# Attention units of two heads by 256 queries, with P times V in the two column halves

## The chip, the core and the metric

The kernel runs on one core of a Trainium2 chip. Its time is the device time in microseconds (us) of that core; a smaller number is better. The kernel before was run three times: 4213.78, 4209.31 and 4176.34 us, median 4209.31 us.

## The reference

Two layers of a hybrid backbone work on 2048 latent tokens, with 256 context tokens as a prefix. Each layer normalises the tokens, projects them to 3100 columns, and feeds three kinds of heads side by side: six Mamba-2 heads (SSD), four gated DeltaNet heads (GDN) and six attention heads over two key/value heads. Their outputs are gated, put side by side and projected back. Everything is fp32. The change is in the attention:

```
def block(qi):
    s = jnp.einsum('bqhgd,bkhd->bhgqk', qi, k).astype(jnp.float32) * scale
    pr = jax.nn.softmax(s, axis=-1).astype(v.dtype)
    return jnp.einsum('bhgqk,bkhd->bqhgd', pr, v)
```

The head dimension is 64. The latent queries attend to all 2304 keys (18 tiles of 128); in the first layer the 256 context queries attend to the 256 context keys as well.

## The kernel before, in words

A layer has three parts. The projection comes first and leaves keys (`khh`, `klo`) and values (`v1`) in SBUF and the rest in DRAM. Then the mixers run: the GDN preparation and its triangular solves (`gdn_pre`, `gdn_solve`), the SSD states and outputs (`ssd_states`, `ssd_out`), and a serial chain over the 18 tiles for GDN (`gdn_chain`), with the attention beside all of them. The output projection ends the layer.

The attention is a list of units. A large unit is one head by 512 queries over 18 key tiles; there are 24 of them in a layer, and in the first layer six small ones (one head by 256 context queries, two key tiles). A unit has two halves. `unit_max` multiplies queries by keys in fp32r (a form of fp32 that TensorE takes in one instruction a product), lets VectorE (DVE) take row maxima (L533), and turns the four columns of maxima into a row of `qm` with plain fp32 products (L541) and a copy by DVE (L542). `unit_main` computes, for each key tile, the scores transposed, with the maxima subtracted, by two products of 512 columns (L562, L563). ScalarE (ACT) takes the exponential into `pe` (L565). Then the product with V accumulates in one PSUM bank, `po` (L556). V has 65 columns a key/value head, of which one is ones, so that the row sums come out as a 65th row of `po`.

Units 0 to 12 of a layer do this last product in plain fp32, which TensorE runs as two instructions. Units 13 to 23 split instead: ACT casts `pe` to fp32r (`ph`, L570), DVE forms the rest (`pl`, L571), V was split beforehand (`vh`), and three fp32r products replace the plain one.

The maxima of the next unit are woven into the scores of this one (`adv` in `attention`). The text puts eight units ahead of `gdn_chain` and the others behind it, but the order on each engine is set by the scheduler, which goes through the whole program with costs of its own and writes a fixed sequence for each engine; each engine then works strictly in its sequence. By that sequence units 0 to 7 stand beside the GDN preparation, the solves and the SSD states, units 8 to 12 beside `ssd_out`, and units 13 to 23 beside `gdn_chain`. GpSimd (POOL) works there on masks (L813, L832) and on the matrices `wb` of the chain (L1044 to L1050), which have two buffers and so wait for the chain step that last read them (L1114). The SSD states (L789) already use products with 64 output columns in the two column halves of the array. Pairs of small numbers such as 128*64 in the profile are the rows and columns of the array that a product uses.

## Time and profile before

| | |
|---|---|
| runs | 4176.34, 4209.31, 4213.78 us |
| profiled execution, span | 4198.6 us |
| TensorE (PE) busy | 95% of the span |
| DVE busy | 68% |
| ACT busy | 44% |
| POOL busy | 36% |
| projection, attention and mixers, output projection (first layer) | 0 to 709, 709 to 1906, 1906 to about 2100 us |
| attention and mixers of the second layer | 2810 to 3992 us |

The profiled execution's own time is its span, 4198.6 us; nothing of the page tells what lies around it. A busy share is a share of the span in which an engine had an instruction under way. The end of a matmul is modelled, so the pace of PE is read from starts, not from ends. A released wait is written as `engine line <- what it waited for`.

### The profile page before, as it was taken

To read this page: it belongs to the slowest core of one execution; us is meant where nothing else is said; L and a number is where in the kernel's file an instruction comes from. 1 tells how busy PE (TensorE), PEld (TensorE's weight loads), DVE (VectorE), ACT (ScalarE), POOL (GpSimd) and SP (SyncE) were. 2 spreads that over 40 slices of the span, in tenths; PEclk is the share of its full clock that TensorE was granted. 3 is DMA by queue.
4 is the path that set the end of the run, shared out by engine and by line. 5 is a ranking of instruction groups with operands and counts; after the bars stand their busy time and mean duration, and the time that the engine had idled before them with its cause. 6 is when DMAs were issued, how large, how long until landed. Compare 5 with 4: busy or idle time off the path is not lost. (4 is left out here: it accounts for less than half of the span.)

```text
span 4198.6 us, 66336 instructions
## 1 busy us (share of the span) xinstructions
PE 4005.7 (95%) x23574; PEld 3044.2 (73%) x23574; DVE 2858.0 (68%) x5652; ACT 1834.2 (44%) x3817; POOL 1500.3 (36%) x1854
## 2 busy tenths in 40 slices
PE   7999999999999999998899999999999999999989
PEld 5899998554566667776678999985545666666667
DVE  6556564889876667875546665648898757677643
ACT  5343432443565545653224434324335645555610
POOL 5121120676465323432313211206755632234300
PEclk9999999999999889999999999999999989898999
DMA  6343432344123333426743434323541233434254
GB/s 198 109 137 103 129 111 93 111 149 165 51 60 89 88 80 83 108 64 214 224 161 118 148 102 128 113 93 103 165 136 55 59 82 77 87 81 97 53 171 155
DMA packets 539143, 477.46 MB, mean 114 GB/s; under 512 B 113784, under 2 KB 476732, under 8 KB 538812
## 3 DMA queue, kind: packets, MB, share of 16 engines
q1 hardware_dynamic: 496956, 437.81, 36.3%
q10 hardware_dynamic: 41856, 35.40, 2.8%
q8 instruction: 187, 3.06, 0.3%
q14 instruction: 144, 1.18, 0.1%
HBM read 328.91 MB, written 144.18 MB: 113 GB/s over the span
## 5 line engine op out<-in xcount | busy, mean ns | idle before, releaser
L565 ACT ACTIVATE pe<-pst 128x512 f32<-128x512 f32 (+1 forms) x876 | 511.7, 594 | 713.7 <-PE pst L563 690.2
L533 DVE TENSOR_REDUCE mx<-pq 128x1 f32<-128x512 f32 (+1 forms) x972 | 594.4, 626 | 135.2 <-PE pq L531 130.8
L531 PE MATMUL pq<-khh,q 128*128 128x512 f32 (+1 forms) x972 | 473.9, 512 | 26.7 <-DVE mx L533 24.8
L556 PE MATMUL po<-pe,v 128*65 128x512 f32 x960 | 487.8, 597 | 1.1 <-ACT os__12118 L579 1.0
L562 PE MATMUL pst<-q,khh 128*128 128x512 f32 (+1 forms) x876 | 433.5, 495 | 16.9 <-DVE mx L533 15.8
L455 PE MATMUL ps<-lo,wh 128*128 128x384 f32 (+2 forms) x1296 | 441.2, 340 | 0.0
L455 PE MATMUL ps<-hi,wl 128*128 128x384 f32 (+2 forms) x1296 | 441.0, 340 | 0.0
L455 PE MATMUL ps<-hi,wh 128*128 128x384 f32 (+2 forms) x1296 | 440.9, 340 | 0.0
L563 PE MATMUL pst<-qm,klo 65*128 65x512 f32 (+1 forms) x876 | 359.1, 411 | 0.0
L401 PE MATMUL ps<-wh,hi 128*128 128x320 f32 (+1 forms) x1120 | 354.3, 318 | 1.9 <-DVE hi L365 1.8
L571 DVE TENSOR_TENSOR pl<-pe,ph 128x512 fp32r<-128x512 f32 x396 | 301.2, 765 | 76.4 <-ACT ph L570 58.6
L401 PE MATMUL ps<-wl,hi 128*128 128x320 f32 (+1 forms) x1120 | 350.3, 314 | 0.0
L401 PE MATMUL ps<-wh,lo 128*128 128x320 f32 (+1 forms) x1120 | 349.7, 315 | 0.7 <-DVE lo L366 0.7
L531 PEld LDWEIGHTS pq<-khh,q 128*128 128x128 f32 x972 | 190.1, 198 | 176.6 <-issue 65.1
L376 DVE TENSOR_TENSOR wl<-wt,wh 128x1024 fp32r<-128x1024 f32 (+3 forms) x144 | 175.8, 1250 | 159.5 <-ACT wh L375 159.3
L556 PE MATMUL po<-ph,vh 128*65 128x512 f32 x792 | 274.7, 429 | 0.6 <-ACT ph L570 0.6
L562 PEld LDWEIGHTS pst<-q,khh 128*128 128x128 f32 x876 | 172.9, 197 | 127.1 <-issue 53.3
L570 ACT CAST ph<-pe 128x512 fp32r<-128x512 f32 x396 | 242.6, 619 | 47.0 <-PE po L556 22.1
L455 PEld LDWEIGHTS ps<-lo,wh 128*128 128x128 f32 x1296 | 244.0, 188 | 10.7 <-issue 0.4
L455 PEld LDWEIGHTS ps<-hi,wl 128*128 128x128 f32 x1296 | 243.4, 188 | 10.4
L455 PEld LDWEIGHTS ps<-hi,wh 128*128 128x128 f32 x1296 | 243.5, 188 | 10.2
L1044 POOL TENSOR_TENSOR wb<-cst,dsc 64x512 f32<-64x512 f32 x72 | 92.8, 1289 | 423.6 <-issue 225.1
(585 smaller groups left out, 8849.4 us busy)
## 6 DMA issues: line engine op xcount, KB each, us to landing
wt<-in_w_in_dram SPq DMA_DIRECT2D x72, 512.0 KB
acv<-pre_d SPq DMA_DIRECT2D x68, 512.0 KB
wmt<-in_w_mod_dram SPq DMA_DIRECT2D x48, 512.0 KB
pre_d<-pre SPq DMA_DIRECT2D x34, 512.0 KB
kqc<-kt_d SPq DMA_DIRECT2D x68, 256.0 KB
wt<-in_w_in_dram SPq DMA_DIRECT2D x24, 668.0 KB
wt<-in_w_in_dram SPq DMA_DIRECT2D x24, 640.0 KB
q<-qt_d SPq DMA_DIRECT2D x48, 256.0 KB
```

Source lines behind the costliest of these rows:

```text
L376: nc.vector.tensor_tensor(out=wl[:, ks, :], in0=wt, in1=wh[:, ks, :].bitcast(F32), op=ALU.subtract)
L401: nc.tensor.matmul(ps, hh[:, k, a], ww[:, k, :], start=(n == 0), stop=(n == 3 * KD - 1))
L455: nc.tensor.matmul(ps, ww[:, k, m * P:(m + 1) * P], hh[:, k, s0:s0 + sn], start=(n == 0), stop=(n == 3 * KD - 1))
L531: nc.tensor.matmul(pq[:, :n], q2[:, u * P:(u + 1) * P], khh[:, kvh, k0t * P + a:k0t * P + a + n], start=True, stop=True)
L533: nc.vector.tensor_reduce(mx[:, i:i + 1], pq[:, :n], axis=AX.X, op=ALU.max)
L556: nc.tensor.matmul(po[0:65, :qn], v[:, kt, vs], p[:, :qn], start=(kt == k0t and j == 0), stop=(kt == k1t - 1 and j == len(ops) - 1))
L562: nc.tensor.matmul(pt[:, :qn], khh[:, kvh, ks], q2[:, :qn], start=True, stop=False)
L563: nc.tensor.matmul(pt[:, :qn], klo[:, kvh, ks], qm[:, :qn], start=False, stop=True)
L565: nc.scalar.activation(out=pe[:, :qn], in_=pt[:, :qn], func=AF.Exp, scale=0.125)
L570: nc.scalar.copy(out=ph, in_=pe)
L571: nc.vector.tensor_tensor(out=pl, in0=pe, in1=ph.bitcast(F32), op=ALU.subtract)
L1044: nc.gpsimd.tensor_tensor(out=wb[dk[d], d, :, :, cS[d]].rearrange("p c h n -> p (c h) n"), in0=cc("ident")[dk[d], None, dk[d]].to_broadcas ...
```

## The change

A unit is now two heads (`pr`, heads 2pr and 2pr+1) by 256 queries (`QN`), still 24 large ones a layer, with three small ones in the first. Scores are four products of 256 columns a key tile (L589, L590) in place of two of 512. P times V is plain fp32 everywhere: the casts, the subtractions and `vh` are gone. Each head's product has 64 output columns and goes to one half of the array's columns and of the PSUM bank's partitions (L575). Products are gathered into visits: once four key tiles are pending, three are multiplied in one go, which are six products, placed behind the score product just issued. The column of ones is gone from V. Row sums are formed by a second pair of half-column products with a matrix of ones (L565), but not for every key tile: `how` names for each one whether TensorE sums it (P) or it is first added to others on GpSimd (G) or DVE (V), so that the sum takes one product pair. In units 0 to 7 (`early`) seven key tiles are added on GpSimd and eleven go to TensorE; in the others (`late`) five are added on GpSimd, ten on DVE, and three go to TensorE. The row of maxima is turned with one fp32r product a column block (L543), negated in the reduction, and copied by ACT; the copy of the queries for `qm` by GpSimd is now a DMA. `pe` has nine buffers where it had four.

```
-                nm = ap_.tile([P, 4], F32, name="nm")
...
+                    nc.vector.tensor_reduce(nmz[:, j, :, 64:65], mx[:, j, :, 0:len(pieces)], axis=AX.X, op=ALU.max, negate=True)
...
-                    nc.tensor.matmul(pm[64:65, u * P:(u + 1) * P], nm[:, u:u + 1], ident, start=True, stop=True)
-                nc.vector.tensor_copy(qm[64:65, :qn], pm[64:65, :qn])
+                        nc.tensor.matmul(pm[0:65, (2 * j + u) * P:(2 * j + u + 1) * P], nmz[:, j, u, :], identr, start=True, stop=True)
+                nc.scalar.copy(out=qm[64:65].rearrange("p j n -> p (j n)"), in_=pm[64:65, :])
...
-                    ops = [(v1, pe)] if ph is None else [(vh[0], ph), (vh[1], ph), (vh[0], pl)]
-                    for j, (v, p) in enumerate(ops):
-                        nc.tensor.matmul(po[0:65, :qn], v[:, kt, vs], p[:, :qn], start=(kt == k0t and j == 0),
-                                         stop=(kt == k1t - 1 and j == len(ops) - 1))
+                def sums(src):
+                    for j in range(2):
+                        mm = nc.tensor.matmul(po[half[j], QN:2 * QN], ones, src[:, j, :], start=False, stop=(done[0] == n_pl - 1))
+                        if done[0] == 0:
+                            after(mm, first[j])
+                    done[0] += 1
+
+                def visit(n, behind):
+                    with tc.high_priority():
+                        for v in range(n):
+                            kt, pe = pend.pop(0)
+                            for j in range(2):
+                                mm = nc.tensor.matmul(po[half[j], 0:QN], v1[:, kt, kvh[j] * 64:kvh[j] * 64 + 64], pe[:, j, :],
+                                                      start=(kt == k0t), stop=False)
...
+                            if plan[kt - k0t] == "P":
+                                sums(pe)
...
-                    nc.tensor.matmul(pt[:, :qn], khh[:, kvh, ks], q2[:, :qn], start=True, stop=False)
-                    nc.tensor.matmul(pt[:, :qn], klo[:, kvh, ks], qm[:, :qn], start=False, stop=True)
-                    pe = ap_.tile([P, 512], F32, name="pe", bufs=4)
+                    for j in range(2):
+                        js = slice(j * QN, (j + 1) * QN)
+                        nc.tensor.matmul(pt[:, js], khh[:, kvh[j], ks], q2[:, j, :], start=True, stop=False)
+                        last_mm = nc.tensor.matmul(pt[:, js], klo[:, kvh[j], ks], qm[:, j, :], start=False, stop=True)
+                    pe = ap_.tile([P, 2, QN], F32, name="pe", bufs=9)
...
-                        nc.scalar.copy(out=ph, in_=pe)
-                        nc.vector.tensor_tensor(out=pl, in0=pe, in1=ph.bitcast(F32), op=ALU.subtract)
...
+                        eng = nc.gpsimd if e == "G" else nc.vector
+                        if e in acc:
+                            eng.tensor_tensor(out=acc[e], in0=acc[e], in1=pe, op=ALU.add)
...
+                    if len(pend) >= 4:
+                        visit(3, last_mm)
...
+                def early(k):
+                    return "G" if k % 2 == 0 and k < 14 else "P"
+
+                def late(k):
+                    return "P" if k > 14 else "G" if k % 3 == 1 else "V"
```

The sequence of PE beside `ssd_out`, before (pst are scores, pq the products for maxima, pt an SSD transpose):

```order
L556 MATMUL po<-pe,v_352 65x512
L562 MATMUL pst<-q_15900,khh 128x512
L563 MATMUL pst<-qm,klo 128x512
L556 MATMUL po<-pe,v_352 65x512
L562 MATMUL pst<-q_16093,khh 128x512
L563 MATMUL pst<-qm,klo 128x512
L556 MATMUL po<-pe,v_352 65x512
```

and now, at the same place:

```order
L532 MATMUL pq<-khh,q_17052 128x512
L532 MATMUL pq<-khh,q_17052 128x256
L589 MATMUL pst<-q_16786,khh 128x256
L590 MATMUL pst<-qm,klo 128x256
L589 MATMUL pst<-q_16786,khh 128x256
L590 MATMUL pst<-qm,klo 128x256
L575 MATMUL po<-pe,v_352 64x256 x6
L906 MATMUL pt<-cst,t_10226 128x128 x3
```

The products with V stood one by one between scores; now six stand together. In the whole sequence 1740 half-column products with V and 716 with ones stand in 420 unbroken runs (291 visits were written), and the number of places where consecutive matmuls use the array in different divisions goes from 1083 to 1747.

The sequence of DVE beside `ssd_out`, before (t, m and sq are tiles of `ssd_out`, mx the maxima):

```order
L839 TENSOR_TENSOR m_9398<-m_9398,pd 128x384
L845 TENSOR_TENSOR t_9406<-po_9430,ecum 128x192
L845 TENSOR_TENSOR t_9407<-po_9430,ecum 128x192
L861 TENSOR_SCALAR sq<-sq 128x1
L533 TENSOR_REDUCE mx<-pq 128x1
L840 TENSOR_TENSOR m_9398<-m_9398,ee 128x384
L533 TENSOR_REDUCE mx<-pq 128x1
```

and now:

```order
L875 TENSOR_TENSOR m_9846<-m_9846,pd 128x384
L881 TENSOR_TENSOR t_9854<-po_9903,ecum 128x192
L897 TENSOR_SCALAR sq<-sq 128x1
L881 TENSOR_TENSOR t_9855<-po_9903,ecum 128x192
L600 TENSOR_TENSOR accV<-pe 128x512
L876 TENSOR_TENSOR m_9846<-m_9846,ee 128x384
L534 TENSOR_REDUCE mx<-pq 128x1
L899 TENSOR_SCALAR t_9761<-t_9761,sq 128x384
L597 TENSOR_TENSOR accV<-accV,pe 128x512
```

The additions of a late unit now stand between the operations of `ssd_out` and the maxima.

The sequence of POOL beside `gdn_chain`, before:

```order
L1050 TENSOR_TENSOR wb_13755<-kqc_13740,er_13741 64x8x64
L522 CAST qm_18209<-q2_18207 64x512
L1044 TENSOR_TENSOR wb_13901<-cst_63,dsc_7169 64x8x64
L1047 TENSOR_TENSOR wb_13901<-acv_13888,kdc_7168 64x8x64
L1050 TENSOR_TENSOR wb_13901<-kqc_13886,er_13887 64x8x64
```

and now:

```order
L597 TENSOR_TENSOR accG_19268<-accG_19268,pe_19315 128x512
L1080 TENSOR_TENSOR wb_15031<-cst_63,dsc_7152 64x8x64
L1083 TENSOR_TENSOR wb_15031<-acv_15018,kdc_7151 64x8x64
L1086 TENSOR_TENSOR wb_15031<-kqc_15016,er_15017 64x8x64
L1080 TENSOR_TENSOR wb_15031<-cst_63,dsc_7152 64x8x64
L1083 TENSOR_TENSOR wb_15031<-acv_15018,kdc_7151 64x8x64
L1086 TENSOR_TENSOR wb_15031<-kqc_15016,er_15017 64x8x64
L1181 TENSOR_TENSOR ox0_14932<-op__14934,ox0_14932 128x256
L1181 TENSOR_TENSOR ox1_14933<-op__14934,ox1_14933 128x256
L597 TENSOR_TENSOR accG_19268<-accG_19268,pe_19360 128x512
```

The copies of the queries are gone, and additions of one unit stand ahead of and behind the group that builds `wb` for the next chain step.

## Rows read from the trace of the kernel before

**Rows 1.** The page: span, and busy us and instructions of each engine.

```profile
span 4198.6 us, 66336 instructions
...
PE 4005.7 (95%) x23574; PEld 3044.2 (73%) x23574; DVE 2858.0 (68%) x5652; ACT 1834.2 (44%) x3817; POOL 1500.3 (36%) x1854
```

**Rows 2.** Windows: start:end length, busy us of PE, PEld, DVE, ACT, POOL; clock, DMA.

```profile
709.00:1080.00 371.00, 338.74 (x1646) 186.76 (x1646) 322.19 (x722) 145.50 (x317) 218.66 (x319) 0.98 0.42 130
1080.00:1340.00 260.00, 257.01 (x1129) 159.60 (x1127) 199.86 (x432) 153.69 (x425) 170.87 (x192) 1.00 0.22 60
1340.00:1906.00 566.00, 545.57 (x4180) 395.20 (x4178) 406.69 (x764) 314.53 (x614) 199.36 (x171) 0.91 0.38 86
2810.00:3992.00 1182.00, 1122.88 (x6791) 728.69 (x6789) 900.84 (x1824) 594.00 (x1290) 549.36 (x643) 0.93 0.35 90
```

**Rows 3.** PE groups by form: count, busy us, mean ns, idle before with releaser.

```profile
L556 PE MATMUL po<-pe,v 128*65 128x512 f32 x936 | 481.5, 603 | 1.1 <-ACT os__12118 L579 1.0
...
L556 PE MATMUL po<-ph,vh 128*65 128x512 f32 x792 | 274.7, 429 | 0.6 <-ACT ph L570 0.6
...
L556 PE MATMUL po<-pl,vh 128*65 128x512 f32 x396 | 173.8, 439 | 4.3 <-DVE pl L571 3.0 <-DMA acv<-pre_d 1.1
...
L541 PE MATMUL pm<-cst,nm 128*1 128x128 f32 x408 | 56.6, 283 | 5.1 <-DVE nm L536 3.5 <-DVE zn L420 1.6
```

**Rows 4.** Timeline of PE, one product of plain fp32: start us, us, instructions.

```profile
768.05 1.02 PE L556 MATMUL po<-pe,v 128*65 128x512 f32 x2
```

**Rows 5.** Timeline of PE in the projection, 256 and then 512 columns in fp32r.

```profile
120.01 0.28 PE L455 MATMUL ps<-hi,wl 128*128 128x256 f32 x1
120.12 0.28 PE L455 MATMUL ps<-hi,wh 128*128 128x256 f32 x1
...
121.63 0.39 PE L455 MATMUL ps<-hi,wh 128*128 128x512 f32 x1
121.86 0.39 PE L455 MATMUL ps<-lo,wh 128*128 128x512 f32 x1
```

**Rows 6.** Timeline of PE, products in column halves (L789): four instructions.

```profile
942.29 0.66 PE L776 MATMUL pt<-cst,xb 128*128 128x128 f32 x4
942.88 0.55 PE L789 MATMUL pst<-xd,bn 128*64 128x192 f32 x4
943.36 0.86 PE L556 MATMUL po<-pe,v 128*65 128x256 f32 x3
```

**Rows 7.** Timeline of PE, the same line with eight instructions.

```profile
970.33 0.87 PE L789 MATMUL pst<-xd,bn 128*64 128x192 f32 x8
971.13 0.66 PE L776 MATMUL pt<-cst,xb 128*128 128x128 f32 x4
971.54 0.48 PE L562 MATMUL pst<-q,khh 128*128 128x512 f32 x1
```

**Rows 8.** Timeline of PE, the eight instructions of a maxima row.

```profile
597.18 1.03 PE L541 MATMUL pm<-cst,nm 128*1 128x128 f32 x8
```

**Rows 9.** DVE groups by form, window 1080 to 1340.

```profile
L840 DVE TENSOR_TENSOR m<-m,ee 128x384 f32<-128x384 f32 x36 | 27.9, 776 | 0.2
...
L839 DVE TENSOR_TENSOR m<-m,pd 128x384 f32<-128x384 f32 x36 | 19.5, 542 | 0.6 <-ACT ee L838 0.5
...
L542 DVE CAST qm<-pm 1x512 fp32r<-1x512 f32 x5 | 3.4, 689 | 6.5 <-PE pm L541 6.5
L536 DVE TENSOR_SCALAR nm<-nm 128x4 f32<-128x4 f32 x5 | 3.4, 683 | 0.2
```

**Rows 10.** DVE groups by form, whole span.

```profile
L571 DVE TENSOR_TENSOR pl<-pe,ph 128x512 fp32r<-128x512 f32 x396 | 301.2, 765 | 76.4 <-ACT ph L570 58.6 <-PE po L556 13.0 <-ACT Z L1106 1.7
```

**Rows 11.** POOL groups by form, whole span.

```profile
L813 POOL TENSOR_TENSOR m<-cst,sp 128x768 f32<-128x768 f32 x34 | 50.3, 1478 | 32.0 <-PE py L856 32.0
...
L1211 POOL TENSOR_TENSOR zs<-zs,rc 128x384 f32<-128x384 f32 x34 | 36.8, 1081 | 293.1 <-DMA zs<-zt_d 164.2 <-DMA bg<-in_b_mod_dram 26.4 <-PE psd L1223 21.8
```

**Rows 12.** Waits of all engines: us in total, times, longest.

```profile
POOL wb L1044 <- PE p L1114: 195.3, 20, 25.6
```

More of the change, by code (lines that the diff above doesn't have):

```diff
@@ L35 @@
 GT = 768
+QN = 256
 def rev(t):
@@ L260, in hybrid_kernel @@
         klo = kv.tile([65, HK, NTOK], F32R, name="klo")
-        v1 = kv.tile([P, NT, 129], F32, name="v1")
+        v1 = kv.tile([P, NT, P], F32, name="v1")
         gates = lay.tile([P, NT, 28], F32, name="gates", bufs=1)
@@ L385, in hybrid_kernel @@
                 for bi, (kind, c0, w, arg) in enumerate(blocks):
-                    if g == 0 and bi == 3:
-                        nc.gpsimd.tensor_copy(v1[:, :, 64:65], cc("ones")[:, None, 0:1].to_broadcast([P, NT, 1]))
                     wh, wl = load_w(c0, w) if g or bi else w_first
@@ L493, in hybrid_kernel @@
             ap_ = splx.enter_context(tc.tile_pool(reuse_waits="tile", name="ap", bufs=2))
[L494 to L495 removed]
+            apz = splx.enter_context(tc.tile_pool(reuse_waits="tile", name="apz", bufs=1))
             ps_s = bx.enter_context(tc.tile_pool(reuse_waits="tile", name="ps_s", bufs=3, space=PSUM))
@@ L572, in unit_main @@
-                    pend.append((kt, pe, ph, pl))
-                    if len(pend) > (3 if sp else 1):
-                        pv()
-                    yield
-                while pend:
-                    pv()
-                os_ = ap_.tile([65, 512], F32, name="os_", bufs=1)
-                nc.scalar.copy(out=os_[:, :qn], in_=po[0:65, :qn])
-                ob, sb_ = (0, 64) if kvh == 0 else (1, 0)
-                nc.sync.dma_start(sm_d[None, HQ * q0 + h * qn:HQ * q0 + (h + 1) * qn], os_[sb_:sb_ + 1, :qn])
@@ new lines, in unit_main @@
+                    nc.scalar.activation(out=pe.rearrange("p j n -> p (j n)"), in_=pt, func=AF.Exp, scale=0.125)
+                    e = plan[kt - k0t]
+                    if e != "P":
+                        eng = nc.gpsimd if e == "G" else nc.vector
+                        if e in acc:
+                            eng.tensor_tensor(out=acc[e], in0=acc[e], in1=pe, op=ALU.add)
+                        elif e in held:
+                            acc[e] = ap_.tile([P, 2, QN], F32, name="acc" + e)
+                            eng.tensor_tensor(out=acc[e], in0=held[e], in1=pe, op=ALU.add)
+                        else:
+                            held[e] = pe
@@ new lines, in unit_main @@
+                    pend.append((kt, pe))
+                    if len(pend) >= 4:
+                        visit(3, last_mm)
+                    yield
+                if pend:
+                    visit(len(pend), last_mm)
+                with tc.high_priority():
+                    for e in held:
+                        sums(acc.get(e, held[e]))
+                os_ = ap_.tile([P, 512], F32, name="os_")
+                nc.scalar.copy(out=os_, in_=po)
+                Q0, w = (0, LC) if q0 < LC else (LC + (q0 - LC) // 512 * 512, 512)
@@ L583, in unit_main @@
+                for j in range(2):
+                    f0 = HQ * Q0 + (h0 + j) * w + q0 - Q0
+                    nc.sync.dma_start(sm_d[None, f0:f0 + QN], os_[64 * j:64 * j + 1, QN:2 * QN])
+                nc.sync.dma_start(mx_d[640 + h0 * 64:768 + h0 * 64, q0:q0 + QN], os_[:, 0:QN])
                 yield
@@ L623, in attention @@
             def attention():
-                big = [(h, LC + qb * 512, 512, 0, NT) for qb in range(LX // 512) for h in range(HQ)]
-                small = [] if last else [(h, 0, LC, 0, TC) for h in range(HQ)]
+                big = [(pr, LC + qb * QN, 0, NT) for qb in range(LX // QN) for pr in range(HQ // 2)]
+                small = [] if last else [(pr, 0, 0, TC) for pr in range(HQ // 2)]
                 sb, ss_ = [{} for _ in big], [{} for _ in small]
@@ L649, in attention @@
                 for i, un in enumerate(big):
-                    if i == 13:
-                        for _ in range(2):
-                            vh.append(spl.tile([P, NT, 129], F32R, name=f"vh{len(vh)}", bufs=1))
-                        nc.scalar.copy(out=vh[0], in_=v1)
-                        nc.vector.tensor_tensor(out=vh[1], in0=v1, in1=vh[0].bitcast(F32), op=ALU.subtract)
-                    spn = () if i < 13 else range(NT)
                     nxt = ms[i:i + 1] + mb[i + 1:i + 2]
-                    left = (21 + 3) * (i + 1 < len(big)) + 3 * (i < len(small))
+                    left = 24 * (i + 1 < len(big)) + 8 * (i < len(small))
                     done = 0
-                    for j, _ in enumerate(unit_main(*un, sb[i], spn)):
+                    for j, _ in enumerate(unit_main(*un, sb[i], early if i < 8 else late)):
                         want = left * (j + 1) // (NT - 4)
@@ L664, in attention @@
                     if i < len(small):
-                        for _ in unit_main(*small[i], ss_[i]):
+                        for _ in unit_main(*small[i], ss_[i], early):
                             pass
```

73 lines of the change are left out of this document (39 added, 34 removed).

## The prediction

> **What bounds the kernel now.** I read the page first. TensorE (PE) is busy in 95% of a span of 4198.6 us, and no other engine in more than 68% [rows 1]. Then the windows by stage, since these shares are means. The attention runs beside three different partners in each layer. In the first layer these are 709 to 1080 (GDN preparation, solve and SSD states, units 0 to 7), 1080 to 1340 (`ssd_out`, units 8 to 12) and 1340 to 1906 (`gdn_chain`, units 13 to 23). In these stages PE is busy 91%, 99% and 96%, and VectorE (DVE) 87%, 77% and 72% [rows 2]. The reader is to see that PE ends first-hand nearly everything, but that in the first two stages DVE stands close behind. A microsecond taken from PE is worth a microsecond in the third stage, and only as much as DVE leaves in the first two. The second layer's mixers, 2810 to 3992, look alike: PE 95%, DVE 76% [rows 2]. The projections aren't touched.
>
> **The pace of PE.** A busy PE overlaps its neighbours, so I take paces from starts. A product of P with V in plain fp32 is two instructions; the pair takes 1.02 us, of which the last alone is 0.60, so that one follows the other at about 0.43 us and the product costs 0.86 [rows 3, 4]. A fp32r product of 512 columns costs 0.23 us, one of 256 columns 0.11 [rows 5]. Thus 936 instructions of plain fp32 cost 402 us (24 short ones of the small units some 5 more), and 792 + 396 split ones 273 us [rows 3]: 680 us in all go.
>
> **What comes.** The SSD states show products in the two column halves: 192 columns, plain fp32. Four instructions (two products) are followed by the next work after 0.48 us, eight (four products) after 0.80 us [rows 6, 7]. So one more product costs 0.16 us, where one of 192 columns alone would cost 2 x 0.43 x 192/512 = 0.32. The halves do run side by side. At 256 columns two products together cost 0.43 us. There are 870 key tiles (24 x 18 in each layer, and 3 x 2), which makes 374 us, and 358 pairs of sums (96 for units 0 to 7 and 80 for the others in each layer, 6 for the small ones), 154 us.
>
> A run of half-column products pays for its beginning and end. In the row of four, 0.48 less 2 x 0.16 leaves 0.16 us. At the entry, four transposes before such a run take 0.59 us, and 0.41 before an undivided product [rows 6, 7], up to 0.18 more. So a run costs 0.16 to 0.34 us. I take 0.2, nearer the lower end, since a part of the 420 runs borders on work that is divided already: 84 us, between 67 and 143. The Trainium skill (TensorEngine Tiling (Array Packing), Key Properties) says that changing the tiling mode, not only the tile, drains TensorE. It speaks against this change, whose scores leave the array whole; the rows agree, and only they have a price.
>
> Scores cost the same in four products of 256 as in two of 512 (4 x 0.11 against 2 x 0.23 [rows 5]). The maxima row goes from eight instructions in about 1.0 us [rows 8] to four fp32r instructions of 128 columns, which lie between half and all of 0.11 us each; I take 0.35 us a unit. There are 51 units by 408 / 8 [rows 3]: 30 us less.
>
> The sum for PE is -680 + 374 + 154 + 84 - 30 = **-98 us**. By unit it is about -1.4 us for units 0 to 7 (twelve sum pairs eat most of it), -4.4 for 8 to 12, and -1.35 for 13 to 23.
>
> **The other engines.** The split's 396 subtractions at 0.765 us [rows 10] leave DVE, all beside `gdn_chain`, as do the casts on ACT. Per unit DVE loses the copy of the maxima row and the negation, 0.69 + 0.68 us [rows 9], but units 8 to 23 bring nine additions each. The two DVE operations of 128x384 beside `ssd_out` bound their price: with one operand in PSUM it is 0.54 us, with both in SBUF 0.78 us [rows 9]. At 512 columns that is 0.72 to 1.03; I take 0.72 to 0.97, below the end because the subtraction, also from SBUF, took 0.765 [rows 10]. POOL gains six (units 0 to 7) or four additions a unit; between 1.08 us at 384 columns and 1.48 at 768 [rows 11] I take 1.25. ACT's new copy and the larger output copy stand where ACT is busy 39 to 59% [rows 2], and the DMAs that replace POOL's copies of the queries are issued one unit ahead; both cost nothing while that holds. If a query load came late, the whole unit would wait.
>
> Now the stages. Beside `ssd_out` a unit takes 52 us, with 40 us of DVE and 34 of POOL [rows 2]. After the change PE needs 47.6, DVE 40 - 1.4 + 9 x (0.72 to 0.97) = 45 to 47.3, and POOL 39. Two engines at 95 to 99% that feed each other don't both run full, so I count half of 5 x 4.4 us: 11 us a layer. In the first stage a unit takes 46 us, DVE 40 of it and POOL 27, which becomes 35; of 8 x 1.4 I count half, 5.5 us. Beside `gdn_chain` DVE and ACT are relieved, so all of 11 x 1.35 us counts, divided by the granted clock of 0.91 [rows 2]: 16 us. That is 32.5 us a layer, **65 us in all**. The profiled execution is 4198.6 us, 10.7 below the median of the runs, 4209.3. Taken from the span the sum gives 4134; taken from the median **4144 us**, which I forecast.
>
> **The rivals.** *PE stays alone in front.* If DVE packs its work (it is busy 87% over 371 us in the first stage [rows 2]), all of the 98 us counts, 102 with the clock in the third stage: 4107 us. For it: PE's idle time put down to DVE is small, 3.5 us before the maxima rows [rows 3]. Against it: what DVE must do beside `ssd_out` grows just where PE shrinks. Chance 0.20.
>
> *The vector engines take the gain.* If the additions cost the upper price, the first two stages stay as long as they are, and only the third gives 2 x 16 us: 4177 us. For it speaks that L840 needs 0.78 us where L839, of the same size, needs 0.54 [rows 9], while POOL is busy 66% [rows 2]. The Trainium skill (SBUF — State Buffer, SBUF: two separate sides) has the rule: DVE and GpSimd share a port pair, and a DVE operation with two SBUF inputs and a GpSimd operation that reads SBUF lock each other out for a whole instruction. The two rows agree with it. By it the additions are dearer on both engines than an operation alone. Chance 0.25.
>
> *Slower: GpSimd's queue beside the chain.* An addition now stands behind the six `wb` operations, the first of which waits for a chain step: 195.3 us in 20 waits, up to 25.6 [rows 12]. The sum over GpSimd's five tiles ends a unit on PE, which takes work strictly in order. It decides once such a wait outlasts the four key tiles between the last addition (k = 13) and the unit's end: 4 x 51/18, about 11 us. If half of the 22 units lose 10 us each, 110 us come back: 4144 + 110 = 4254 us. Against it: nine `pe` buffers, and most `wb` groups fall elsewhere in a unit. Chance 0.15.
>
> *The halves don't overlap when they accumulate.* Then 1228 pairs cost 0.43 us more each, 528 us: about 4640 us. Rows 6 and 7 speak against it [rows 6, 7]. Chance 0.03.
>
> *Narrow products carry a fixed cost.* The starts are read to 0.01 us; that much on each of 1740 more score products is 17 us: 4161 us. Chance 0.02. The Trainium skill (TensorEngine Tiling (Array Packing), Instruction Overhead) gives some 60 cycles to each matmul, whatever its width. An estimate by that page, at 2.4 GHz, is 25 ns each, 43 us, and a time of 4187 us; 0.11 against 0.23 us disagrees, as 256 columns cost half of 512 [rows 5].
>
> **How the numbers follow.** The forecast keeps 0.35. The range that holds 8 of 10 reaches from 4075 (the first rival with the runs of products at their lower price gives 4090, and the three runs before differ by more than the rest) to 4225 (the upper price of the runs of products, 143 us, on top of the second rival gives 4236); outside lie the fourth rival, most of the third and a little below, together 0.2. Within 1%, which is about what a measurement of this kernel tells from no change, means 4167 to 4251. Faster: 0.30 of the forecast's 0.35, the first rival's 0.20, 0.05 of the second's and 0.01: 0.56. Slower: 0.13 of the third's, 0.03, and 0.02 of the second's: 0.18. The same: 0.26.
>
> **What would show it.** In the profile after, six half-column products should take about 1.3 us with starts in pairs, and a run's next work begin about 0.16 us later than its products explain. PE's busy time should fall, most between the end of the SSD states and the chain. There DVE should be above 90% and name itself before PE's maxima products; if it is below 85% while PE is full, the first rival holds. Additions on DVE above 0.9 us mean the second. Waits of the sum product (L565) for `accG` in the chain stage, above 5 us each, mean the third. The forecast is wrong in kind if PE's work falls by less than 50 us, or if the granted clock beside the chain moves by more than 0.03 from 0.91, which I take as unchanged.

## The result and the profile after

The changed kernel is **slower**: 4370.1 us (median of 4 runs, 4355.2 to 4414.0) against 4206.4 for the kernel before in the same rounds, a ratio of 1.041 with a 95% interval of 1.035 to 1.047. The forecast was 4144 us, and 4370 lies above its whole range.

First, the page of the profile after (span; busy us of each engine, share, instructions) and its mean granted clock. They answer to [rows 1].

```profile
span 4353.1 us, 74170 instructions
...
PE 4074.3 (94%) x27862; PEld 3275.1 (75%) x27862; DVE 2796.2 (64%) x5296; ACT 1633.6 (38%) x3461; POOL 1770.6 (41%) x2024
...
core 0: 4353.1 us, clock 0.929
```

The kernel before has this line for the clock:

```profile
core 0: 4198.6 us, clock 0.958
```

PE is still busy 94% of the span. That share hides the result, and an account of three parts shows it. **Idle** is the span less PE's busy time. **Clock loss** is the span times one less the granted clock, since the clock has two levels, 2.4 and 1.2 GHz, and time at the lower one does half the work. Time at the lower level in which PE stood idle is in both, so half of it, by the clock's record and PE's instructions, is **counted twice** and is put back. What is left is **work**, PE's busy time as it would be at the full clock.

| us | span | idle | clock loss | counted twice | work |
|---|---|---|---|---|---|
| before | 4198.6 | 192.9 | 176.3 | 17.5 | 3846.9 |
| after | 4353.1 | 278.8 | 309.1 | 29.7 | 3794.9 |
| difference | +154.5 | +85.9 | +132.8 | +12.2 | -52.0 |

PE's work did fall. About four times as much came back, most of it through the clock. The windows by stage say where (length, then busy us of PE, PEld, DVE, ACT, POOL, granted clock, DMA share, GB/s). They are the stages of [rows 2], moved to where they now begin and end.

```profile
703.00:1111.00 408.00, 362.70 (x2610) 246.30 (x2608) 330.65 (x682) 148.28 (x306) 275.41 (x353) 0.92 0.40 123
1111.00:1425.00 314.00, 286.20 (x1573) 202.73 (x1572) 246.77 (x469) 161.90 (x444) 205.48 (x206) 0.86 0.18 52
1425.00:1993.00 568.00, 538.21 (x4950) 416.21 (x4949) 338.63 (x626) 207.99 (x428) 240.57 (x207) 0.89 0.39 90
2880.00:4147.00 1267.00, 1160.62 (x8951) 845.95 (x8949) 887.67 (x1696) 491.86 (x1115) 682.61 (x733) 0.89 0.33 87
```

The stage beside `ssd_out` took 260 us with PE busy 99% at a clock of 1.00 [rows 2]; it now takes 314, with PE busy 91% at 0.86, and DVE at 79%. The stage ahead of it went from 371 to 408 us. By these windows the chain's stage stayed (566 and 568). From the projection's end to the chain's first product it is 631 us before and 727 after in the first layer, 595 and 713 in the second: 96 and 118 us more, with nearly the same attention work in it, counted by score products (13.4 and 13.0 units before, 13.6 and 13.4 now). Counted by products for the maxima it is more: 14.9 and 14.7 units now against 13.6 and 13.0, so DVE has the reductions of 1.3 and 1.7 more units in it. What that alone costs, no run shows.

PE's groups by form, which answer to [rows 3] (count, busy us, mean ns, idle before):

```profile
L575 PE MATMUL po<-pe,v 128*64 128x256 f32 x3480 | 558.8, 441 | 0.0
...
L565 PE MATMUL po<-pe,cst 128*64 128x256 f32 x1112 | 173.0, 390 | 0.0
...
L543 PE MATMUL pm<-identr,nmz 128*65 128x128 f32 x204 | 30.9, 241 | 2.2 <-DVE nmz L537 1.4 <-DVE mx L534 0.6
```

The products of P and V (L575), the sums (L565) and the halved maxima row (L543) never wait for long. The waiting is done by the products ahead of them. What PE waits for, in the whole span (us in total, times, longest us), first after, then before:

```profile
PE pq L532 <- DVE mx L534: 53.8, 56, 4.7
PE pst L589 <- DVE mx L534: 43.2, 38, 6.2
```

```profile
PE pq L531 <- DVE mx L533: 24.8, 19, 4.7
PE pst L562 <- DVE mx L533: 15.8, 22, 2.1
```

Both score tiles (`pst`) and tiles for the maxima (`pq`) take the same PSUM slots, and both wait until DVE has reduced an older `pq`: 97 us instead of 41, which is 56 of the 85.9 us of added idle time. How such a wait looks stands in the timeline beside `ssd_out`, first of DVE, then of PE (start us, duration, line, tile, count, idle before with its releaser).

```profile
1303.93 3.34 DVE L852 SCALAR_TENSOR_TENSOR m<-cst,sp,m 128x128 f32<-128x128 f32 x5
1307.19 1.27 DVE L534 TENSOR_REDUCE mx<-pq 128x1 f32<-128x512 f32 x2
```

```profile
1306.12 0.29 PE L590 MATMUL pst<-qm,klo 65*128 65x256 f32 x1
1307.92 1.18 PE L532 MATMUL pq<-khh,q 128*128 128x512 f32 x2 [1.52 <-DVE mx L534]
1308.90 0.41 PE L589 MATMUL pst<-q,khh 128*128 128x256 f32 x1
```

In DVE's sequence five operations of the SSD stand ahead of the reduction, so the slot comes free at 1307.9 and PE stands still for 1.52 us. In the clock's record the level falls at 1308.2. The windows on both sides of it (PEclk is the third value from the end):

```profile
1296.00:1308.20 12.20, 10.68 (x71) 7.72 (x69) 7.34 (x14) 7.85 (x23) 8.57 (x9) 1.00 0.29 83
1308.20:1315.00 6.80, 6.79 (x40) 4.91 (x39) 6.80 (x13) 2.08 (x5) 5.39 (x5) 0.75 0.00 0
```

There are 20 such falls between 703 and 1425, and in the 5 us ahead of each PE had been idle, 0.8 to 2.8 us in all. Not all such idle time is followed by a fall: of 84 other stretches of 5 us there, at the full clock and not just ahead of a fall, nine had 0.8 us or more, and the mean is 0.24 us. Between the first SSD product and the chain, the clock fell 7 times in the two layers before the change and 39 times after it; in the whole span 41 and 80 times.

### The profile page after: what moved, and what is told of

Read it like the earlier page. It is cut to its first block, busy times and chain, and to the rows that moved or that the text cites. A ratio compares the mean times of both kernels' runs of the same rounds, so it can differ in the third digit from the quotient of the medians.

```text
span 4353.1 us, 74170 instructions
## 1 busy us (share of the span) xinstructions
PE 4074.3 (94%) x27862; PEld 3275.1 (75%) x27862; DVE 2796.2 (64%) x5296; ACT 1633.6 (38%) x3461; POOL 1770.6 (41%) x2024
## 5 line engine op out<-in xcount | busy, mean ns | idle before, releaser
L592 ACT ACTIVATE pe<-pst 128x512 f32<-128x512 f32 x870 | 512.3, 596 | 842.8 <-PE pst L590 822.4
L589 PE MATMUL pst<-q,khh 128*128 128x256 f32 x1740 | 539.3, 329 | 51.0 <-DVE mx L534 43.2
L575 PE MATMUL po<-pe,v 128*64 128x256 f32 x3480 | 558.8, 441 | 0.0
L590 PE MATMUL pst<-qm,klo 65*128 65x256 f32 x1740 | 490.4, 301 | 0.0
L532 PE MATMUL pq<-khh,q 128*128 128x512 f32 (+1 forms) x972 | 411.1, 463 | 71.5 <-DVE mx L534 53.8
L589 PEld LDWEIGHTS pst<-q,khh 128*128 128x128 f32 x1740 | 358.5, 206 | 155.8 <-DVE mx L534 62.8
L590 PEld LDWEIGHTS pst<-qm,klo 65*128 65x128 f32 x1740 | 361.1, 208 | 12.9 <-issue 1.7
L597 POOL TENSOR_TENSOR accG<-accG,pe 128x512 f32<-128x512 f32 x176 | 232.1, 1319 | 318.1 <-ACT pe L592 298.6
L575 PEld LDWEIGHTS po<-pe,v 128*64 128x64 f32 x3480 | 241.4, 154 | 154.4 <-issue 64.8
L597 DVE TENSOR_TENSOR accV<-accV,pe 128x512 f32<-128x512 f32 x256 | 215.3, 841 | 55.1 <-ACT pe L592 52.8
```

Source lines behind the costliest of these rows:

```text
L532: nc.tensor.matmul(pq[:, :n], q2[:, j, u * P:(u + 1) * P], khh[:, kvh, k0t * P + a:k0t * P + a + n], start=True, stop=True)
L575: mm = nc.tensor.matmul(po[half[j], 0:QN], v1[:, kt, kvh[j] * 64:kvh[j] * 64 + 64], pe[:, j, :], start=(kt == k0t), stop=False)
L589: nc.tensor.matmul(pt[:, js], khh[:, kvh[j], ks], q2[:, j, :], start=True, stop=False)
L590: last_mm = nc.tensor.matmul(pt[:, js], klo[:, kvh[j], ks], qm[:, j, :], start=False, stop=True)
L592: nc.scalar.activation(out=pe.rearrange("p j n -> p (j n)"), in_=pt, func=AF.Exp, scale=0.125)
L597: eng.tensor_tensor(out=acc[e], in0=acc[e], in1=pe, op=ALU.add)
```

## The experiments

All fifteen runs in one table. The times are medians, the ratio is to the kernel before, with its 95% interval. Idle, clock loss, counted twice (2x) and work come from each kernel's one profiled execution, as above. That execution can lie off the median: those of e11 and e13 were the slowest of their ten, those of e3 and e7 the fastest of their four. The granted clock is on record for every execution, so the median clock loss of all of them stands beside it; for the changed kernel it is 330 us, for the kernel before 176 (17 executions beside e12). The edits below are abridged.

| run | us | ratio | idle | clock loss | median of all | 2x | work |
|---|---|---|---|---|---|---|---|
| `e1_no_adds` | 4265.0 | 1.017 (1.011 to 1.024) | 218.9 | 272.8 | 264 | 22.3 | 3793.2 |
| `e2_short_max` | 4242.7 | 1.011 (1.006 to 1.016) | 210.6 | 267.5 | 256 | 19.4 | 3786.9 |
| `e3_visit_one` | 4436.4 | 1.054 (1.045 to 1.062) | 195.3 | 333.3 | 381 | 25.5 | 3882.9 |
| `e4_row_only` | 4153.9 | 0.990 (0.984 to 0.995) | 198.9 | 183.4 | 166 | 12.1 | 3798.2 |
| `e5_no_pool_adds` | 4314.3 | 1.025 (1.019 to 1.031) | 232.8 | 323.6 | 319 | 23.9 | 3781.9 |
| `e6_no_dve_adds` | 4325.2 | 1.029 (1.024 to 1.034) | 244.9 | 307.0 | 303 | 22.1 | 3794.6 |
| `e7_runs_before` | 4262.7 | 1.015 (1.009 to 1.021) | 245.6 | 220.3 | 260 | 43.0 | 3814.0 |
| `e8_pairs_late` | 4199.6 | 1.001 (0.998 to 1.004) | 204.6 | 214.1 | 222 | 12.8 | 3791.2 |
| `e9_one_no_adds` | 4407.3 | 1.053 (1.047 to 1.059) | 151.6 | 395.6 | 405 | 14.0 | 3861.9 |
| `e10_adds_on_before` | 4327.8 | 1.032 (1.028 to 1.035) | 290.8 | 285.2 | 290 | 54.8 | 3800.1 |
| `e11_light_vector` | 4202.7 | 1.001 (0.998 to 1.004) | 179.5 | 274.8 | 244 | 12.7 | 3785.7 |
| `e12_row_again` | 4151.7 | 0.990 (0.986 to 0.994) | 194.4 | 161.5 | 170 | 16.0 | 3800.6 |
| `e13_seven_pe` | 4203.7 | 1.002 (0.998 to 1.005) | 236.4 | 245.2 | 220 | 40.5 | 3785.7 |
| `e14_sums_on_pe` | 4475.2 | 1.068 (1.063 to 1.073) | 236.2 | 245.5 | 253 | 22.0 | 4004.1 |
| `e15_six_pe` | 4376.5 | 1.043 (1.038 to 1.048) | 273.2 | 351.2 | 342 | 28.0 | 3793.7 |

Work is good to about 15 us: that far apart are kernels with the same products on PE (e4, e10, e12 and e13: 3785.7 to 3800.6; the changed kernel, e1, e2, e5, e6, e11 and e15: 3781.9 to 3794.9). e7, with the products of e4 in another order, lies 13 us above the first group.

### The additions: e1, e5, e6, e14

```diff
-    acc[e] ... eng.tensor_tensor(out=acc[e], in0=acc[e], in1=pe, op=ALU.add)   # e1: both engines
+    if e == "G" and e in held: pass     # e5: POOL's left out; e6: "V", VectorE's
-    return "G" if k % 2 == 0 and k < 14 else "P"          # e14: early(k) and late(k)
+    return "P"
```

e1: 

> Left out: the additions on VectorE and GpSimd (the row sums lack the key tiles marked G and V but the first of each); the exponent's scale is 0.001, so that no sum is zero. TensorE's products are the same in number as in the changed kernel (4355 us in its profiled run, 4370 median; before 4206). Theory 1 (TensorE starves on VectorE's maxima because the additions fill VectorE and lock its port): idle time of PE beside ssd_out falls from 28 to under 10 us, the granted clock there from 0.86 back to over 0.95, and the time to 4220 to 4270. Theory 2 (the gathered visits starve TensorE: scores and maxima come in bursts with nothing of P times V between them): at most 30 us less, and the stage of units 0 to 7, which has no VectorE additions, stays near 408 us. Theory 3 (half-column products lower the granted clock by themselves): clock stays at 0.86 to 0.90 and the time within 40 us of 4370.

e5: 

> The changed kernel with POOL's additions of P tiles left out (VectorE's stay; the sums then lack those tiles; exponent scaled by 0.001 so that sums stay finite). Leaving out both engines' additions gave 4265 us against 4370. Theory 1, VectorE's queue: maxima stand behind additions in VectorE's order, so TensorE's slots come free late; then this run gains little, 4340 to 4370, and TensorE's idle time in the stage between the first SSD product and the chain stays near the 63 and 73 us of the two layers. Theory 2, POOL: its additions of 1.35 us each delay the SSD steps on POOL for which VectorE waits, and lengthen VectorE's own operations; then most of the 105 us come back here, 4270 to 4300, the idle falls to about 46 and VectorE's 128x384 product goes from 861 ns towards 803.

e6: 

> The changed kernel with VectorE's additions of P tiles left out (POOL's stay; sums lack those tiles; exponent scaled by 0.001). Theory 1 (VectorE's queue): most of the 105 us come back here, 4270 to 4310. Theory 2 (POOL): 4340 to 4370. As VectorE adds only in units 8 to 23, theory 1 expects the gain late in the stage before the chain and beside the chain, theory 2 none there.

e14: 

> The changed kernel complete, but with every sum on TensorE and none added on VectorE or POOL: per layer 6 x 8 + 13 x 16 = 256 more pairs of sum products, 0.43 us each, 222 us of TensorE's work in both layers. Leaving the additions out gave 4265 us; if only TensorE's work is added to that, 4265 + 222 = 4490. If products that lengthen the runs also keep TensorE from idling and its clock up, less of it shows: 4380 to 4440.

Without any addition the kernel takes 4265 us, 105 less than the changed one: in the profiled executions 60 us of idle time and 36 of clock loss, at the same work; by the clocks of all executions the clock's part is 65. The time lies in the range of e1's theory 1, but beside `ssd_out` (1080 to 1359) PE still idles 16 us at a clock of 0.92, where under 10 us and over 0.95 were expected: the additions are a part of the cause. Without POOL's alone it gains 56 us, without DVE's alone 45; together 101, so the two add up. As e5 and e6 name them, theory 1 (VectorE's queue) and theory 2 (POOL) were each meant to take it all, and both fall as stated. How POOL's additions act is less clear. Here are DVE's groups beside `ssd_out`, after, then in e5, then the mask operation in e1 (1080 to 1359) and in e11 (1052 to 1332), which have no additions (count, busy us, mean ns, idle before):

```profile
L852 DVE SCALAR_TENSOR_TENSOR m<-cst,sp,m 128x128 f32<-128x128 f32 x108 | 61.5, 630 | 5.9 <-POOL m L849 5.9
L534 DVE TENSOR_REDUCE mx<-pq 128x1 f32<-128x512 f32 x82 | 54.2, 679 | 17.6 <-PE pq L532 17.4
L597 DVE TENSOR_TENSOR accV<-accV,pe 128x512 f32<-128x512 f32 x40 | 37.5, 938 | 6.7 <-ACT pe L592 6.7
L876 DVE TENSOR_TENSOR m<-m,ee 128x384 f32<-128x384 f32 x36 | 31.0, 861 | 0.1
```

```profile
L534 DVE TENSOR_REDUCE mx<-pq 128x1 f32<-128x512 f32 x75 | 49.8, 680 | 13.9 <-PE pq L532 13.5
L854 DVE SCALAR_TENSOR_TENSOR m<-cst,sp,m 128x128 f32<-128x128 f32 x102 | 48.0, 531 | 3.6 <-POOL m L851 3.6
L599 DVE TENSOR_TENSOR accV<-accV,pe 128x512 f32<-128x512 f32 x35 | 30.5, 872 | 4.0 <-ACT pe L592 3.9
L878 DVE TENSOR_TENSOR m<-m,ee 128x384 f32<-128x384 f32 x36 | 28.6, 794 | 0.3
```

```profile
L847 DVE SCALAR_TENSOR_TENSOR m<-cst,sp,m 128x128 f32<-128x128 f32 x104 | 57.5, 612 | 6.9 <-POOL m L844 6.9
L847 DVE SCALAR_TENSOR_TENSOR m<-cst,sp,m 128x128 f32<-128x128 f32 x102 | 70.1, 750 | 7.6 <-POOL m L844 7.6
```

In e5 DVE's operations whose tensors lie in SBUF are shorter by 7 to 16% (630 to 531, 938 to 872, 861 to 794 ns), while the reduction that reads PSUM stays (679 and 680). The Trainium skill (SBUF — State Buffer, SBUF: two separate sides) says that a DVE operation with two SBUF inputs and a GpSimd operation that reads SBUF hold one port pair against each other. The rows agree with it in that the first kind varies and the reduction does not. But that POOL's additions make the difference is not shown: without any addition the same mask operation took 612 ns in e1 and 750 in e11.

e14, a complete computation, settles what the additions replace: the sums on TensorE cost 209 us of work (222 were estimated) and give back 43 us of idle time and 64 of clock loss in the profiled executions. It is 105 us slower than with the additions. So the additions are the better of the two ways, and still cost 105 us.

### The maxima: e2, e11

```diff
-    nc.vector.tensor_reduce(mx[:, j, u, i:i + 1], pq[:, :n], axis=AX.X, op=ALU.max)
+    nc.vector.tensor_reduce(mx[:, j, u, i:i + 1], pq[:, :64], axis=AX.X, op=ALU.max)
```

e2: 

> Left out: seven eighths of each maxima reduction (64 of 512 columns); the exponent's scale is 0.001. Everything else as in the changed kernel. Theories 1 and 2 (starvation by VectorE's maxima, whatever makes them late): PE's idle time and the falls of the clock beside units 0 to 12 go nearly away, clock over 0.96 there, time about 4370 - 2 x (40 + 50) = 4190 or less. Theory 3 (half-column products lower the clock): the clock beside ssd_out stays under 0.90 although PE idles less than 10 us there, time over 4300.

e11 (with e1's edit): 

> The changed kernel with the additions left out and the maxima taken over 64 of 512 columns (output wrong in both respects, exponent scaled by 0.001): TensorE's work is the changed kernel's, 3771 us at full clock, and VectorE and POOL are lighter than in the kernel before. If the load on these two is the whole cause, idle and clock loss fall to the kernel before's 188 and 176 us or below: 4100 to 4140. If the products in runs leave TensorE idle of themselves, 4180 to 4240, as with the additions alone or the maxima alone lightened (4265, 4243).

Shorter reductions bring 127 us: VectorE's work as a whole, not the additions alone, decides how long PE's slots are held. At 4243 us e2 lies in neither of its ranges (4190 or less, over 4300); beside `ssd_out` (1090 to 1402) PE still idles 30 us, at a clock of 0.90. With both lightened, in e11, idle time falls below that of the kernel before (179.5 against 192.9), but the clock loss stays above it, by 98 us in the profiled execution, which was the slowest, and by 68 in the median of all. 4203 us lies in the range of the second theory, products that leave TensorE idle of themselves, yet that is not what happened, since the idle time is gone: the load on VectorE and POOL explains all of the added idle time, but not all of the clock loss.

### Runs of six products: e3, e9, e7, e13, e15

```diff
-    if len(pend) >= 4: visit(3, last_mm)
+    if len(pend) >= 2: visit(1, last_mm)        # e3; e9: with e1's edit too
-    if len(pend) > (3 if sp else 1): pv()       # e7: the old units with e4's row
+    if not sp and len(pend) > 3: three times pv(), the first behind the scores
-    name="pe", bufs=4                           # e13: e4's kernel; e15: 9 to 6 in the changed one
+    name="pe", bufs=7
```

e3: 

> Visits of one key tile (two products and their sums) as soon as two are pending, in place of three as soon as four are. Theory 2 (bursts): PE's idle time on the maxima falls to that of before (about 35 us in the first two stages of a layer), the clock there rises to over 0.95; but the runs of half-column products grow by some 12 a unit, 51 x 12 x 0.2 = 122 us, so the time is 4300 to 4400. Theory 1 (additions): idle time and clock stay as they are beside ssd_out, and the runs come on top: 4450 to 4500. Theory 3: as theory 1.

e9: 

> The changed kernel with both engines' additions left out (sums lack tiles, exponent scaled by 0.001) and with its products done one key tile at a time. The runs of one key tile cost TensorE 91 us at full clock in the run that had the additions (844 runs instead of 426), so its work at full clock should be about 3865 us of the span. Theory A, additions and long runs are together what leaves TensorE idle: idle time and loss by the half clock come back to those of the kernel before, 188 and 176 us, 4210 to 4250 in all. Theory B, the pairs themselves do it (less TensorE work beside the same maxima): they stay above 190 and 260, 4310 and more.

e7: 

> The kernel before with the new maxima row (4154 us), and its plain fp32 products of P and V held back and done three key tiles at a time, as the change does, each run behind the scores of the fourth tile; nothing halved, nothing added on VectorE or POOL. Theory 3, runs: with the products held back TensorE has nothing to do while VectorE is late with a slot, so idle time and falls of the clock come with the runs alone: idle before the chain goes from 34 and 33 us to 50 to 70 per layer, the loss by the half clock from 8 and 5 us to 30 to 60, 4230 to 4300 in all. Rival: the idle time comes from the load on VectorE and POOL, and runs only save changes of format: 12 fewer per unit of 18 key tiles, 13 units, 2 layers, 0.2 us each is 62 us, so 4090 to 4140.

e13: 

> The kernel before with the new maxima row (4152 us) and seven pe buffers in place of four, nothing else. Both runs that put one part of the change into the old units (runs of three key tiles, 4263 us; additions, 4328 us) had seven. If runs and additions are what cost there, this one stays at 4140 to 4170 with 12.7 and 11.5 units between the first SSD product and the chain. If the deeper pool is the cause, because scores may run further ahead and the order written out ahead of time takes more attention work into that stage (14.4 and 16.2 units in those two), it goes to 4200 to 4260.

e15: 

> The changed kernel with six pe buffers in place of nine, nothing else. If the depth of the pool costs, through attention work taken too early into the stage before the chain (13.2 and 12.9 units there), it gets faster, 4280 to 4330, with fewer units in that stage; if additions and runs cost of themselves, 4350 to 4400.

e3 has 844 runs of half-column products in the trace instead of 426, and 88 us more work: 0.21 us a run, where the forecast took 0.2. Its idle time falls by 84 us, and its time, 4436 us, lies between the ranges of theories 2 and 1. So holding the products back does starve PE between runs, but giving it up costs as much and more. e9 leaves out the additions as well. The windows of the two stages, first layer, then second:

```profile
703.00:1337.00 634.00, 604.07 (x4061) 404.51 (x4061) 504.10 (x1095) 302.59 (x736) 380.27 (x492) 0.97 0.34 105
1337.00:1975.00 638.00, 624.46 (x4827) 452.52 (x4828) 275.28 (x537) 203.88 (x417) 169.93 (x163) 0.76 0.35 81
2899.00:3524.00 625.00, 592.96 (x3891) 394.83 (x3890) 480.15 (x1037) 284.51 (x686) 361.32 (x472) 0.94 0.33 100
3524.00:4159.00 635.00, 624.97 (x4824) 452.35 (x4825) 262.42 (x520) 200.68 (x410) 158.75 (x151) 0.75 0.33 79
```

Theory A holds for the idle time before the chain: without additions and without long runs PE is idle 30 us there (634 less 604), where the change had 73 (45 and 28 in its first two windows) and the kernel before 35 [rows 2]. The clock comes back to 0.97 in the first layer, but only to 0.94 in the second. It fails beside the chain, where the clock is 0.76 and 0.75 though PE is busy 98% of the time. Of six falls in the first layer's chain stage, five last 55 to 61 us in the clock's record; after the change a fall lasts 7.7 us on average (2 x 309.1 / 80). So the lowest idle time of all runs (151.6) goes with the highest clock loss (395.6). **The clock loss is not a function of idle time.** Ahead of eleven of e9's twelve falls beside the chain PE had stood idle too, 1.0 to 1.7 us in 5 us; but within these falls it stands idle for 0.2 us at most, and eleven last 38 to 61 us. Beside the chain a fall lasts 3 to 14 us in the changed kernel, 10 to 41 in e3 with its short runs, and up to 31 and 34 in e1 and e11 without the additions; e9 has both, short runs and no additions. Why either of them keeps the clock low, these runs don't show.

e7 came with a deeper `pe` pool, so e13 had to tell the two apart. The pool alone costs 52 us in the old units (4203.7 against 4151.7): the order takes 15.3 and 14.4 units before the chain instead of 13.3 and 12.6, and beside the chain, with less attention left, PE is idle 60 and 52 us in place of 44 and 25. e7 is 59 us above e13, so runs hurt in plain, undivided products too; the 62 us that e7's rival saw saved on changes of format did not come, as the work is not lower (3814.0 against 3785.7). The two profiled executions lie only 10 us apart, but by the clocks of all executions 40 of the 59 us are clock loss (260 against 220). In the changed kernel the depth is worth nothing (e15, 4376.5, in its second range).

### Where it sits, and the row by itself: e8, e4, e12, e10

```diff
-    big = [(pr, LC + qb * QN, 0, NT) for qb in range(LX // QN) for pr in range(HQ // 2)]
+    big = [(h, LC + qb * 512, 512, 0, NT) for qb in range(2) for h in range(HQ)]              # e8
+    big += [(pr, LC + qb * QN, 0, NT) for qb in range(4, LX // QN) for pr in range(HQ // 2)]
-    nc.vector.tensor_reduce(nm[:, u:u + 1], ...)     # e4, e12: kernel before
+    nc.vector.tensor_reduce(nmz[:, u, 64:65], ..., negate=True)
-    nc.tensor.matmul(pm[64:65, ...], nm[:, u:u + 1], ident, ...)
+    nc.tensor.matmul(pm[0:65, ...], nmz[:, u, :], identr, ...)
+    eng.tensor_tensor(out=acc[e], in0=acc[e], in1=pe, op=ALU.add)    # e10: e4, units 0 to 12
```

e8: 

> The first twelve attention units of each layer as in the kernel before with the new maxima row (one head by 512 queries, plain fp32 products tile by tile), the last twelve as in the changed kernel (two heads by 256, halves, runs of six, additions on VectorE and POOL). If the change loses only in the stage before the chain, this stage comes back to about 584 and 541 us and the chain's stage is as the changed kernel's, 567 and 566: 4154 - 46 + 15 = 4123 us, 4100 to 4150, at least as good as the maxima row alone. Rival: the pairs cost as much beside the chain as they save (the half clock takes 60 us a layer there in every kernel), 4150 to 4200.

e4: 

> The kernel before with the row of maxima alone taken from the change (fp32r product, negation in the reduction, copy by ScalarE, queries for qm by DMA). By the sum of the prediction PE loses 30 us and VectorE 1.4 us a unit; if that part does what it says: 4206 - 20 to 35 = 4170 to 4186. If the move of the copy to ScalarE or the DMA costs something (late qm): 4206 or more.

e12: 

> The kernel before with the new maxima row alone, once more in five rounds: 4154 us were measured, 0.9897 of the kernel before. Expected 4140 to 4170; if the gain was chance, 4190 to 4210.

e10: 

> The kernel before with the new maxima row (4154 us), and units 0 to 12 of each layer also do the change's additions on POOL (units 0 to 7: six; 8 to 12: four, and nine on VectorE), whose results nobody uses; products and scores as before. Theory A, the additions cost what they cost in any form: the stage before the chain grows from 584 and 541 us by about 40 each, 4220 to 4250. Rival: they hurt only where TensorE's own work has shrunk; as it stands here it covers them, 4150 to 4180.

With old units in the first half, the time before the chain is 611 us with 12.5 units of attention in it, against 631 with 13.4 before and 727 with 13.6 after the change. The windows of e8, first layer, before and beside the chain:

```profile
701.00:1312.00 611.00, 567.29 (x2651) 337.48 (x2650) 497.45 (x1115) 299.79 (x742) 385.20 (x492) 0.97 0.36 109
1312.00:1911.00 599.00, 563.74 (x4937) 437.28 (x4937) 351.59 (x652) 211.97 (x429) 239.56 (x207) 0.85 0.41 88
```

So the loss sits in the units that run beside GDN preparation and `ssd_out`. But the pairs don't pay beside the chain either: e8 is 48 us slower than e12, with 53 us more clock loss, and its work is 9 us lower, where the forecast's 1.35 us for each of eleven units in two layers gives 30. The time lies in the range of that expectation's rival. One difference between e8 and e12 is not tested: e8 has nine `pe` buffers, e12 four. What the deeper pool did in e13, more attention before the chain, is not seen in e8 (12.5 and 12.2 units; e12 13.3 and 12.6); instead about one unit a layer stands behind the output projection's first product, outside these windows.

The maxima row alone makes the kernel **1% faster** than before, in two measurements (0.990; 0.986 to 0.994 in five rounds); e4 came out below its range of 4170 to 4186. Of the 52 us of work that the change takes off PE, it gives 46 (3846.9 to 3800.6). It is the best version found.

e10 went further than either expectation. Against e13, with the same pool, the additions in units 0 to 12 alone cost 124 us, at work that differs by 14 (3800.1 and 3785.7): 54 us of idle time and 40 of clock loss in the profiled executions, and 69 of clock loss by the medians of all. Theory A holds, with too small a figure, and not only by its path: the stage before the chain grew from 682 to 757 us, but it also took 16.5 units instead of 15.3. The additions hurt in the old form too, where PE's own work has not shrunk.

## Why the prediction was wrong

**The failed step** is the one that went from PE's work to the stages: "Two engines at 95 to 99% that feed each other don't both run full, so I count half", together with the granted clock "which I take as unchanged". It priced waiting by mean loads, and the clock not at all. The forecast named its own condition, a clock beside the chain that moves by more than 0.03; beside the chain it went from 0.91 to 0.89, but beside `ssd_out` from 1.00 to 0.86. I had looked for the movement in the wrong stage. In place of the 16.5 us a layer that the first two stages were to give, they cost 96 and 118, and the runs put this on idle time of PE behind late reductions (e1, e2 and e11) and on the clock.

- *Most of PE's prices held.* Six half-column products took 1.51 us to the modelled end of the last, and 1.30 by starts (7 and 209 ns in turn); a run costs 0.21 (e3) for 0.2; 426 runs for 420.

```profile
1320.70 1.51 PE L575 MATMUL po<-pe,v 128*64 128x256 f32 x12
```

- *The sum for PE was too large*: 52 us came instead of 98. The maxima row alone gave 46 (e12), said 30; its own prices give 33, and by starts its own products took 28 us less in e12. That leaves about 6 us for all the rest, said 68, and 6 is less than work can be told to. 14 us of what is missing is the price of narrow score products, 121 ns where half of a 512-column product is 117, times four in 870 tiles: the fifth rival's mechanism, which I had at 17 us and left out of the sum. The runs take 5 more. Some 40 us are not located.
- *The additions' prices held*: DVE 841 ns over the span and 938 beside `ssd_out` (said 720 to 970), POOL 1319 (said 1250). Beside `ssd_out` DVE's passed 0.9 us, the forecast's sign of its second rival. The prices were right and their effect wrong: they act on when a slot comes free. e1 puts that at 105 us, e2 shows it for the reductions.
- *DVE named itself before PE's products*, as the forecast wanted to see, 97 us instead of 41. It was at 79% beside `ssd_out`, not above 90%. The forecast's test for its first rival, DVE below 85% while PE is full, was met in its first half alone: PE was busy 91%. Neither engine was full, a case that the test did not have: where operations of the SSD stood in a row ahead of a reduction on one, the other starved. PE's busy time, which was to fall, rose by 69 us.
- *The vector engines take the gain* had the right mechanism and ended it at zero. It went past zero: to 85.9 us of idle time came 132.8 through the clock (12.2 of it counted twice).
- *GpSimd's queue beside the chain* is not what happened. No wait of the sum products for `accG` stands among PE's waits, and the chain's stage, from its first product to the output projection's first, got shorter by 7 and 27 us (574 to 567, 593 to 566). That the time came out slower is no credit to it.
- *The halves don't overlap* is refuted by the 7 and 209 ns.
- Beside the chain the forecast gave 16 us a layer; 7 and 27 came, which may be chance: e4 and e12, the same kernel, differ by more than 20 us in this stage of the first layer. The loss is all before it: 96 and 118 us, where a gain of 16.5 a layer was forecast.

What is shown: the place (e8), the additions' share (e1, e5, e6, e10), that additions and long runs together account for the added idle time before the chain (e9). Left open: what keeps the clock low for 55 us and more beside the chain in e9, how POOL's additions act, and some 40 us of work. No run has the plain fp32 products alone in place of the split ones of units 13 to 23, and none the half-column products alone.

## What to carry to other kernels

Work taken off a full engine is worth something only if the engines that hand it its slots can deliver faster; check the longest in-order burst on them, not their mean load. Where the granted clock moves between two kernels, write the account as idle time, clock loss and work, since a busy share of 95 and one of 94% hid 133 us of clock loss here. And try each part of a bundled change alone: here the smallest part, one row, was the only one tried that paid.

## What was not expected of the hardware

- In the 5 us ahead of every one of 20 falls of TensorE's clock PE had stood idle, 0.8 to 2.8 us in all, such as the 1.52 us above. The Trainium skill (TensorE: Matmul & The Clock Gate, A second HAM failure mode: psum-queue depth-cycling) describes a kernel whose PE idles briefly between groups of products while it cycles through PSUM banks and whose clock goes up and down for it; the waits for slots here are of that kind.
- The clock can stay at its lower level for 55 to 61 us while PE is 98% busy (e9 beside the chain); after the change it came back after 3.4 to 10.2 us beside `ssd_out`, once after 23.9.
- One DVE operation with its tensors in SBUF took 531 ns (e5), 612 (e1), 630 (after) and 750 (e11) beside `ssd_out`, while the reduction from PSUM stayed at 679 to 682 ns in the first three; the additions on POOL alone don't explain it, as e1 and e11 have none.
- A score product of 256 columns took 121 ns by starts, 4 more than half of one of 512 (234).
